# Tree attention: K and Q of heads 16 to 79 laid side by side by GpSimd, 18 output buffers, another order of the products with V

## The chip, the cores and the metric

One core of one Trainium2 chip runs the whole kernel. The metric is device time in microseconds of one execution. The names of the engines are those of the profile: PE is TensorE (matrix products; PEld its weight loads), DVE is VectorE, ACT is ScalarE, POOL is GpSimd, SP is SyncE. POOL also issues most of the DMA transfers.

## What is computed

Attention over 8 x 12 = 96 heads with 512 positions of 64 numbers each, under a mask that is a tree: position i sees itself and its ancestors (parent (i - 1) // 2).

```python
mask = np.zeros((seq, seq))
for i in range(seq):
    mask[i, i] = 1
    parent = i
    while parent > 0:
        parent = (parent - 1) // 2
        mask[i, parent] = 1
scores = np.einsum('bhqd,bhkd->bhqk', Q, K) * scale + (1 - mask) * (-1e9)
weights = np.exp(scores - np.max(scores, axis=-1, keepdims=True))
weights = weights / (np.sum(weights, axis=-1, keepdims=True) + 1e-10)
return np.einsum('bhqk,bhkd->bhqd', weights, V).astype(np.float32)
```

All inputs and the output are fp32 in device memory.

## The kernel before

**Pairs.** The 96 heads are worked as 48 pairs; in a pair, one head lies in partitions 0 to 63 and the other in 64 to 127 wherever the 64 dimensions lie on the partitions. One iteration of the main loop (line 860) takes the scores of pair i ("S": scores1 and scores2), the products with V of pair i - 1 ("V": values and norm), and turns (transposes) K or Q of later pairs ("K", "Q"). Pairs 0 to 7 are turned one by one, pairs from 8 (WIDE) on by two. From pair 8 on K comes in odd iterations and Q in even ones, apart from the first iterations, whose order is written out in FIRST (line 856). There, iteration 6 is 'SKDVQ': scores of pair 6, then K of pairs 8 and 9 is turned. Later, iteration i turns Q of pairs i + 4 and i + 5 if it is even, and K of i + 3 and i + 4 if it is odd. "D" and "A" are the places where VectorE and ScalarE spread V.

**The mask** enters through codes: each score tile begins with a product of two code matrices (L567, L601) that adds a large negative number where the tree forbids, and the product of Q and K is added on top (L574, L612). scores1 makes the 512 queries' scores with the 128 topmost keys (tile s1, exponential into e1), scores2 the rest (tile s2, exponentials into e2). s1, s2 and the output tile ob have one PSUM buffer each, so that the next pair's scores wait for the exponentials of the pair before.

**Loads.** K, Q and V come as bf16 (the DMA casts from fp32) in blocks: K and Q in blocks b of 8 heads (4 buffers each), V in blocks of 16 heads (3 buffers). They are all issued by POOL, in the order of pool_program (line 720), mixed with POOL's share of spreading V (spread_top, spread_pool: copies from the loaded rows vst to the tiles vt, L371) and with the stores (L702). POOL works its list strictly in order; pool(i) only says after which iteration an instruction is put into the program, which fixes which readers of a buffer a new load has to wait for.

**Turning.** A turn brings 8 slots of two heads from rows to columns by products with an identity matrix. For pairs 8 to 39 each slot takes two transposes, one for each head, with 64 columns of the array each (L477 for K, L507 and L538 for Q): 16 of them. For blocks 10 and 11 (heads 80 to 95, pairs 40 to 47) lay_beside has POOL copy a block so that the two heads of each slot lie side by side (L445), and a slot then takes one transpose with 128 columns (L470, L532): 8 of them. VectorE takes the result out of PSUM (L486, L490, L494 for K; L515, L543 for Q).

**Products with V.** values(i) makes 20 products (L662): for each of the two heads four with e1 and two with e2, all with 128 queries, and after both heads the 8 products "halves", with 64 queries each, that end the sums. norm divides (L692, L694) into an output tile "of" of 8 heads. There are NOUT // 2 = 11 of those; a tile is free again when its store has landed.

Of the kernel before, what the change touches and what calls it, by code (L numbers as in the profile page):

```python
# [9 lines left out]

CODE = 2048.0
CODE_ROWS = 40
NOUT = 22
BEHIND = 56


# [21 lines left out]
SELF = (2, 3, 2, 3)  # L38
# [81 lines left out]
def kernel(  # L120
# [7 lines left out]
    nc = tc.nc  # L128
# [33 lines left out]

    consts = ctx.enter_context(tc.tile_pool(name="consts", bufs=1))
    loads = ctx.enter_context(tc.tile_pool(name="loads", bufs=4))
    vloads = ctx.enter_context(tc.tile_pool(name="vloads", bufs=3))
    work = ctx.enter_context(tc.tile_pool(name="work", bufs=4))
    qwork = ctx.enter_context(tc.tile_pool(name="qwork", bufs=2))
# [272 lines left out]
    def lay_beside(name, b):  # L440

        kept = ksts if name == "kst" else qsts
        assert all((name, h) in issued for h in range(KB * b, KB * b + KB))
        sides[name, b] = side = loads.tile([P, KB, 4, D], bf16, name=name)
        return nc.gpsimd.tensor_copy(  # L445
            out=side.rearrange("p (s a) t d -> p s a (t d)", a=2).rearrange(
                "p s a (t d) -> p (s a t) d", t=4
            ).rearrange("p (s a) d -> p s a d", a=2).bitcast(int32),
            in_=kept[b].rearrange("p (a x) t d -> p (x t) a d", a=2).bitcast(int32),
        )  # L450

    def both(name, i, slot):

        side = sides[name, i // 4].rearrange("p h t d -> p (h t d)")
        return side[:, 2 * D * slot:2 * D * slot + 2 * D]

    def slots(st, i):
        return st[2 * i // KB].rearrange("p (g x) t d -> p g (x t) d", x=2)

    def wide_k(i):  # L460
        kp = ktp.rearrange("p u c -> p (u c)")
        st = slots(ksts, i)
        place = [2 * i % KB // 2 + a if i < FAR else i % 4 // 2 + 2 * a for a in range(2)]
        for u in range(2):
            for t in range(4):
                mixed = 64 * MIXED[t] + 32 * u
                leaves = 512 + 64 * LEAVES[t] + 32 * u
                dims = (256, 2), (leaves - mixed, 2), (1, 32)
                if ("kst", i // 4) in sides:
                    nc.tensor.transpose(  # L470
                        out=columns(kp, mixed, *dims),
                        in_=both("kst", i, 8 * (i % 4 // 2) + 4 * u + t),
                        identity=ptile[:, 0:128],
                    )
                    continue
                for a in range(2):
                    nc.tensor.transpose(  # L477
                        out=columns(kp[64 * a:64 * a + 64, :], mixed, *dims),
                        in_=st[:, place[a], 4 * u + t, :],
                        identity=ptile[:, 0:128],  # L480
                    )
# [12 lines left out]
        nc.vector.tensor_copy(  # L494
            out=columns(flat, 0, (320, 4), (128, 2), (1, 64)),
            in_=columns(kp, 512, (128, 4), (64, 2), (1, 64)),
        )

    def wide_q(i):
        qp = qtp.rearrange("p u c -> p (u c)")  # L500
        halves = qp.rearrange("p (b c) -> p b c", b=2)
        st = slots(qsts, i)
        for u in range(2):
            for x, t in enumerate(ORDER):
                c = 256 * u + 64 * x
                for a in range(2):
                    nc.tensor.transpose(  # L507
                        out=halves[64 * a:64 * a + 64, :, c:c + 64],
                        in_=st[:, 2 * i % KB // 2 + a, 4 * u + t, :],
                        identity=ptile[:, 0:128],  # L510
                    )
# [3 lines left out]
        nc.vector.tensor_copy(  # L515
            out=qq[:, :, 0:16, :].rearrange("p b u c -> p b (u c)"), in_=halves
        )
# [3 lines left out]
    def far_q(i):  # L521
        qp = qtp.rearrange("p u c -> p (u c)")
        quarters = qp.rearrange("p (b c) -> p b c", b=4)
        j, last = i // 4, i % 4 // 2
        if not last:
            qqs[j] = qwork.tile([P, 4, 16, 32], bf16, name="qq")
        st = qsts[j].rearrange("p (g x) t d -> p g (x t) d", x=4)
        for u in range(2):
            for x, t in enumerate(ORDER):
                c = 128 * u + 32 * x  # L530
                if ("qst", j) in sides:
                    nc.tensor.transpose(  # L532
                        out=quarters[:, :, c:c + 32], in_=both("qst", i, 4 * (2 * last + u) + t),
                        identity=ptile[:, 0:128],
                    )
                    continue
                for a in range(2):
                    nc.tensor.transpose(  # L538
                        out=quarters[64 * a:64 * a + 64, :, c:c + 32],
                        in_=st[:, a, 4 * (2 * last + u) + t, :],  # L540
                        identity=ptile[:, 0:128],
                    )
        nc.vector.tensor_copy(  # L543
            out=qqs[j][:, :, 8 * last:8 * last + 8, :].rearrange("p b u c -> p b (u c)"),
            in_=quarters,
        )
        if last:
            for b in range(4):
                qTs[4 * j + b] = qqs[j][:, b, :, :].rearrange("p (t u) c -> p t (u c)", t=4)

    def turn(name, i):
        pairs = range(i, i + (2 if i >= WIDE else 1))
        if name == "qst" and i >= FAR:
            pairs = range(i - i % 4, i - i % 4 + 4)
        assert all((name, head(j, a)) in issued for j in pairs for a in range(2)), (name, i)
        level = (i >= WIDE) + (i >= FAR)
        {"kst": (narrow_k, wide_k, wide_k), "qst": (narrow_q, wide_q, far_q)}[name][level](i)
        return i + (2 if i >= WIDE else 1)

# [90 lines left out]
    def values(i):  # L650
# [15 lines left out]
                **flags,  # L666
            )

        def halves(a):
            for t in (0, 1):  # L670
                product(e2, a, t, 1 + SELF[t], 0, 64, start=False, stop=t == 1)
                product(e2, a, t, 1 + t, 64, 128, start=False, stop=t == 1)

        for a in range(2):
            for t in range(4):
                product(e1, a, t, 0, start=t == 0, stop=False)
            for t in (2, 3):
                product(e2, a, t, 1 + t, start=False, stop=False)
            if i == NP - 1:
                halves(a)  # L680
        if i < NP - 1:
            for a in range(2):
                halves(a)

# [35 lines left out]
    def pool_program():  # L720
# [6 lines left out]
            (load_q, 16, 4), (load_rows, 1, "even"), (load_k, 20, 4), (load_rows, 1, "odd"),  # L727
            (load_q, 20, 4), (load_k, 24, 8), (load_q, 24, 4), (load_rows, 2, "upper"),
            (load_q, 28, 4), (load_rows, 2, "leaves0", "leaves1"), (load_k, 32, 8), (load_q, 32, 8),
            (load_rows, 3, "upper"),  # L730
            (spread_pool, (1, "Z0", 8, 16), (1, "Z1", 8, 16), (1, 6, 8, 16), (1, 9, 8, 16)),
            (load_q, 40, 8), (load_k, 40, 8), (load_rows, 3, "leaves0", "leaves1"), (load_q, 48, 8),
            (spread_top, 2), (spread_pool, (2, "Z0", 0, 16), (2, "Z1", 0, 16)), (load_k, 48, 8),
            (spread_pool, (2, "X", 0, 16), (2, "M", 0, 16), (2, "D1", 0, 16)), (spread_top, 3, 0, 12),
            (load_rows, 4, "upper"), (spread_top, 3, 12, 16),
        ]
        loaded, stored = 72, 0
        for h in range(56, NH, KB):
            top = [(spread_top, h // VB + 0)] if h % VB == 8 and 4 <= h // VB + 0 < NH // VB else []
            if top:  # L740
                top.append((spread_pool, (h // VB, "Z0", 0, 16), (h // VB, "Z1", 0, 16)))
            ops += [(load_q, h, KB)] + top + [(load_k, h, KB)]
            if h == 64:
                ops.append((
                    spread_pool, *[(3, part, 0, 16) for part in ("Z0", "Z1", "X", "M", "D1")]
# [22 lines left out]
    def ready(op, i):  # L768
# [2 lines left out]
        if f in (load_k, load_q):  # L771
            return 2 * (i + 3) >= args[0] + args[1] - 4 * KB
        if f is lay_beside:
            return 2 * (i + 3) >= KB * (args[1] + 2) + KB - 4 * KB
        if f is load_v:
            return True
        if f is load_rows:
            return 2 * i >= VB * (args[0] - 2)
        if f is spread_pool:
            return 2 * i >= VB * (args[0][0] + 1 - NV)  # L780
        if f is spread_top:
# [145 lines left out]
```

## Time and profile before

| | |
|---|---|
| median of 3 runs | 134.0 us (133.42 to 134.24) |
| the profiled execution | 133.38 us, its span 131.6 us |
| busy, share of the span | PE 114.4 us (87%), DVE 103.8 (79%), ACT 101.1 (77%), POOL 83.0 (63%) |
| moved, by the instructions' account | 37.94 MB read from HBM, 12.58 MB written: 384 GB/s over the span |
| granted TensorE clock, mean | 0.969 |

The span runs from the first to the last instruction; the time of the execution is 1.8 us longer. Busy shares are means over stages in which different engines set the pace, so they are read together with the rows that say what each instruction waited for. A row of the chain gives a start, a length and a name; a row of the timeline gives a start, a length, the engine, the line, the operation and its tiles, and in brackets the idle time before it and what ended that. "x16" after a row means 16 instructions in one. The waits before DMA issues on POOL often end at the landing of an earlier transfer.

### The profile page before, as it was taken

What the parts mean: (1) busy time and instruction counts of PE and PEld (TensorE: products, weight loads), DVE (VectorE), ACT (ScalarE), POOL (GpSimd) and SP (SyncE); (2) the same over time, 40 slices, a digit from 0 to 9 for tenths busy, and PEclk for the clock granted to TensorE, in tenths of its full rate; (3) what the DMA queues carried; (4) which work ended last, traced back from release to release, by engine and by line L of the source; (5) the groups of instructions that cost most, each with busy time, mean ns of one, the idle gap of its engine ahead of it and who ended that gap; (6) DMA issues with size and microseconds to landing.
All of it is one profiled execution on the core that took longest, in us unless ns stands there. A gap on an engine that the chain in (4) does not pass through costs nothing.

```text
span 131.6 us, 5435 instructions
## 1 busy us (share of the span) xinstructions
PE 114.4 (87%) x2353; PEld 79.7 (61%) x2353; DVE 103.8 (79%) x254; ACT 101.1 (77%) x163; POOL 83.0 (63%) x114
## 2 busy tenths in 40 slices
PE   6788959999999798899998898997998999999900
PEld 2354745676667566577676575675675777775600
DVE  3459859588999998989899879898899977875440
ACT  4279577689799996959996878896898888789900
POOL 6999524454485999994498799944999935002000
PEclk9999996799999999999999999999999999999975
DMA  2999999999999999999999999999999999999991
GB/s 87 244 195 194 200 196 200 201 202 206 203 201 209 207 207 204 210 206 202 209 206 200 306 269 207 293 282 242 330 221 327 246 288 400 403 398 396 395 345 66
DMA packets 28157, 32.25 MB, mean 245 GB/s; under 512 B 1214, under 2 KB 23358, under 8 KB 28134
## 3 DMA queue, kind: packets, MB, share of 16 engines
q0 software_dynamic: 25696, 29.63, 110.7%
q1 hardware_dynamic: 1878, 1.83, 4.0%
q10 hardware_dynamic: 560, 0.46, 1.3%
q8 instruction: 18, 0.29, 0.8%
q14 instruction: 5, 0.04, 0.1%
HBM read 37.94 MB, written 12.58 MB: 384 GB/s over the span
## 4 chain that ended last, share of the span: by engine, by line
DMA 30%; PE 29%; POOL 17%; DVE 13%; issue 4%; ACT 2%; POOLq 0%; ACTq 0%
DMA kst<-in_K_dram 22%; PE ob L662 9%; POOL vt L371 9%; DMA vst<-in_V_dram 8%; PE s L567 4%; DVE of L694 4%; DVE vt L371 3%; PE s L574 3%; POOL kst L244 2%; POOL qst L244 2%; PE s L612 2%; PE s L601 2%; POOL vst L244 2%; PE qtp L532 2%; PE ktp L470 2%
## 5 line engine op out<-in xcount | busy, mean ns | idle before, releaser
L584 ACT ACTIVATE e<-s 128x1024 bf16<-128x1024 f32 x40 | 40.9, 1022 | 13.2 <-PE s L574 12.7
L662 PE MATMUL ob<-vt,e 128*128 128x65 bf16 (+1 forms) x940 | 37.4, 198 | 1.6 <-DVE of L694 1.1
L662 PEld LDWEIGHTS <-e 128*128 128x128 bf16 (+1 forms) x960 | 30.4, 103 | 9.5 <-PE s L612 1.1
L371 POOL COPY vt<-vst 32x512 int32<-32x512 int32 (+4 forms) x44 | 32.5, 740 | 5.2 <-PE ob L662 3.0
L618 ACT ACTIVATE e<-s 128x384 bf16<-128x384 f32 x80 | 34.7, 490 | 0.0
L694 DVE TENSOR_TENSOR of<-ob,rec 128x512 f32<-128x512 f32 x47 | 32.5, 692 | 1.6
L371 DVE COPY vt<-vst 32x1024 bf16<-32x1024 bf16 (+5 forms) x47 | 21.4, 456 | 2.6 <-DMA vst<-in_V_dram 1.8
L692 DVE RECIPROCAL rec<-ob 128x8 f32<-128x8 f32 x47 | 9.6, 205 | 10.7 <-PE ob L662 9.8
L702 POOL DMA_DIRECT2D out_dram<-of x11 | 9.9, 898 | 9.1 <-DVE of L694 8.7
L574 PE MATMUL s<-qq,kq 64*128 64x512 bf16 x80 | 15.3, 377 | 0.0
L612 PE MATMUL s<-qq,kq 64*128 64x160 bf16 (+1 forms) x320 | 14.8, 208 | 0.4 <-issue 0.4
L612 PEld LDWEIGHTS <-kq 64*128 64x128 bf16 x320 | 12.3, 94 | 4.7 <-issue 0.6
L567 PE MATMUL s<-far,codes 40*128 40x512 bf16 x64 | 12.5, 386 | 0.1
L580 ACT ACTIVATE e<-s 128x1024 bf16<-128x1024 f32 x8 | 8.2, 1022 | 5.6 <-PE s L574 5.5
L254 POOL DMA_DIRECT2D qst<-in_Q_dram x12 | 8.4, 704 | 6.3 <-DMA kst<-in_K_dram 3.4
L601 PEld LDWEIGHTS <-codes 40*128 40x128 bf16 x80 | 6.4, 94 | 9.5 <-issue 3.9
L543 DVE COPY qq<-qtp 128x1024 bf16<-128x1024 bf16 x16 | 10.9, 682 | 0.7 <-PE qtp L538 0.7
L254 POOL DMA_DIRECT2D kst<-in_K_dram x11 | 8.4, 764 | 4.3 <-DMA vst<-in_V_dram 1.7
L477 PE MATMUL ktp<-ptile,kst 128*64 128x128 bf16 x256 | 9.9, 220 | 1.2 <-DMA kst<-in_K_dram 0.6
L601 PE MATMUL s<-far,codes 40*128 40x384 bf16 x64 | 10.6, 324 | 0.4 <-ACT e L618 0.3
L371 ACT COPY vt<-vst 32x512 int32<-32x512 int32 (+3 forms) x19 | 10.4, 546 | 0.6 <-DMA vst<-in_V_dram 0.2
L299 POOL DMA_DIRECT2D vst<-in_V_dram x7 | 5.6, 800 | 6.4 <-DMA vst<-in_V_dram 4.5
(56 smaller groups left out, 157.2 us busy)
## 6 DMA issues: line engine op xcount, KB each, us to landing
out_dram<-of POOLq DMA_DIRECT2D x10, 1024.0 KB, 16.4
kst<-in_K_dram POOLq DMA_DIRECT2D x9, 512.0 KB, 14.3
qst<-in_Q_dram POOLq DMA_DIRECT2D x8, 512.0 KB, 16.3
vst<-in_V_dram POOLq DMA_DIRECT2D x12, 256.0 KB, 14.0
vst<-in_V_dram POOLq DMA_DIRECT2D x6, 512.0 KB, 13.0
qst<-in_Q_dram POOLq DMA_DIRECT2D x6, 256.0 KB, 12.1
kst<-in_K_dram POOLq DMA_DIRECT2D x4, 256.0 KB, 10.8
out_dram<-of SPq DMA_DIRECT2D x3, 256.0 KB, 6.0
```

Source lines behind the costliest of these rows:

```text
L254: return nc.gpsimd.dma_start(out=kept[b][:, h0 % KB:h0 % KB + n, :, :].rearrange("p (g x) t d -> p g (x t d)", x=x), in_=src[:, h0 // x:(h ...
L371: return copy(out=dst, in_=src)
L477: nc.tensor.transpose(out=columns(kp[64 * a:64 * a + 64, :], mixed, *dims), in_=st[:, place[a], 4 * u + t, :], identity=ptile[:, 0:128],)
L543: nc.vector.tensor_copy(out=qqs[j][:, :, 8 * last:8 * last + 8, :].rearrange("p b u c -> p b (u c)"), in_=quarters,)
L567: nc.tensor.matmul(out=sp[:, a, :], lhsT=(k1code if i < WIDE else k1wide)[64 * a:64 * a + CODE_ROWS, :], rhs=(q1code, q1wide, q1far)[(i >= ...
L574: nc.tensor.matmul(out=sp[:, a, :], lhsT=keys(i, a, TOP), rhs=qTs[i][64 * a:64 * a + 64, :, :].rearrange("p t c -> p (t c)"), start=False, ...
L584: ) if i < WIDE else nc.scalar.activation(
L601: nc.tensor.matmul(out=flat[:, a, :, :].rearrange("p u (t c) -> p u t c", t=4)[:, :, :, 32 // n:], lhsT=k2wide[64 * a:64 * a + CODE_ROWS, ...
L612: nc.tensor.matmul(out=flat[:, a, :, lo:hi], lhsT=keys(i, a, WTILE2[t]), rhs=qT[64 * a:64 * a + 64, :, lo:hi], start=False, stop=t == 1, s ...
L618: nc.scalar.activation(out=e2s[i % NE][:, a, :, 32:128].rearrange("p t (r u) -> p t r u", u=n), in_=flat[:, a, :, :].rearrange("p u (t r) ...
L662: nc.tensor.matmul(out=ob[lo:hi, a, 65 * t:65 * t + 65], lhsT=e[:, a, PLACE[t], lo:hi], rhs=vt[vtile[tile_v][0]][:, head(i, a) % VB, vtile ...
L694: nc.vector.tensor_tensor(out=ofs[j][:, h0:h1 + 1:head(i, 1) - head(i, 0), :, :], in0=o4[:, a:a + n, :, 0:D], in1=rec[:, a:a + n, :, :].to ...
```

## The change

It has four parts. POOL lays K and Q of blocks 2 to 9 (heads 16 to 79) side by side too, into a pool "beside" of its own with two buffers for each of K and Q; blocks 2 and 3 in two half copies each. All pairs from 8 on are then turned by 8 transposes with 128 columns. The copies stand at given places of POOL's list, behind loads and spreads; the load of Q of heads 56 to 63 moves ahead of some spreads and of the upper rows of V block 4, and the conditions under which entries of the list may be put into the program are adapted. The output tiles go from 11 to 9. In values, for pairs 8 to 46, the half products come first (and start the sums), and the products with 128 queries follow.

```diff
-NOUT = 22
+NOUT = 18
...
+    beside = ctx.enter_context(tc.tile_pool(name="beside", bufs=2))
...
-        sides[name, b] = side = loads.tile([P, KB, 4, D], bf16, name=name)
-        return nc.gpsimd.tensor_copy(
...
+        sides[name, b] = side = beside.tile([P, 16, 2, D], bf16, name=f"{name}side")
+        if KB * b >= 2 * FAR:
+            return nc.gpsimd.tensor_copy(
+                out=side.bitcast(int32),
+                in_=kept[b].rearrange("p (a x) t d -> p (x t) a d", a=2).bitcast(int32),
+            )
+        for m in range(2):
+            nc.gpsimd.tensor_copy(
+                out=side[:, 8 * m:8 * m + 8, :, :].bitcast(int32),
+                in_=kept[b][:, 4 * m:4 * m + 4, :, :].rearrange(
+                    "p (a x) t d -> p (x t) a d", a=2
+                ).bitcast(int32),
+            )
...
     def wide_k(i):
...
-                for a in range(2):
-                    nc.tensor.transpose(
-                        out=columns(kp[64 * a:64 * a + 64, :], mixed, *dims),
-                        in_=st[:, place[a], 4 * u + t, :],
-                        identity=ptile[:, 0:128],
-                    )
+                nc.tensor.transpose(
+                    out=columns(kp, mixed, (256, 2), (leaves - mixed, 2), (1, 32)),
+                    in_=both("kst", i, 8 * (i % 4 // 2) + 4 * u + t),
+                    identity=ptile[:, 0:128],
+                )
...
-        def halves(a):
+        def halves(a, start=False):
             for t in (0, 1):
-                product(e2, a, t, 1 + SELF[t], 0, 64, start=False, stop=t == 1)
-                product(e2, a, t, 1 + t, 64, 128, start=False, stop=t == 1)
-
+                for tile_v, lo in ((1 + SELF[t], 0), (1 + t, 64)):
+                    product(
+                        e2, a, t, tile_v, lo, lo + 64, start=start and t == 0,
+                        stop=not start and t == 1,
+                    )
+
+        first = i >= WIDE and i < NP - 1
+        if first:
+            for a in range(2):
+                halves(a, True)
         for a in range(2):
             for t in range(4):
-                product(e1, a, t, 0, start=t == 0, stop=False)
+                product(e1, a, t, 0, start=t == 0 and not first, stop=False)
             for t in (2, 3):
-                product(e2, a, t, 1 + t, start=False, stop=False)
+                product(e2, a, t, 1 + t, start=False, stop=first and t == 3)
             if i == NP - 1:
                 halves(a)
-        if i < NP - 1:
+        if i < NP - 1 and not first:
...
             (load_q, 28, 4), (load_rows, 2, "leaves0", "leaves1"), (load_k, 32, 8), (load_q, 32, 8),
-            (load_rows, 3, "upper"),
+            (lay_beside, "kst", 2), (lay_beside, "qst", 2), (load_rows, 3, "upper"),
             (spread_pool, (1, "Z0", 8, 16), (1, "Z1", 8, 16), (1, 6, 8, 16), (1, 9, 8, 16)),
-            (load_q, 40, 8), (load_k, 40, 8), (load_rows, 3, "leaves0", "leaves1"), (load_q, 48, 8),
+            (load_q, 40, 8), (load_k, 40, 8), (lay_beside, "kst", 3), (lay_beside, "qst", 3),
+            (load_rows, 3, "leaves0", "leaves1"), (load_q, 48, 8),
             (spread_top, 2), (spread_pool, (2, "Z0", 0, 16), (2, "Z1", 0, 16)), (load_k, 48, 8),
-            (spread_pool, (2, "X", 0, 16), (2, "M", 0, 16), (2, "D1", 0, 16)), (spread_top, 3, 0, 12),
+            (lay_beside, "kst", 4), (lay_beside, "qst", 4),
+            (spread_pool, (2, "X", 0, 16), (2, "M", 0, 16), (2, "D1", 0, 16)),
+            (load_q, 56, 8), (lay_beside, "qst", 5), (lay_beside, "kst", 5), (spread_top, 3, 0, 12),
             (load_rows, 4, "upper"), (spread_top, 3, 12, 16),
...
-            ops += [(load_q, h, KB)] + top + [(load_k, h, KB)]
+            beside = [(lay_beside, name, h // KB - 2) for name in ("qst", "kst")]
+            ops += ([(load_q, h, KB)] + beside if h > 56 else []) + top + [(load_k, h, KB)]
...
         if f is lay_beside:
-            return 2 * (i + 3) >= KB * (args[1] + 2) + KB - 4 * KB
+            return args[1] < 4 or i >= 4 * args[1] - 8
...
         if f is load_rows:
-            return 2 * i >= VB * (args[0] - 2)
+            return i >= {4: 12, 5: 17}.get(args[0], 8 * (args[0] - 2))
```

wide_q and far_q change like wide_k: one transpose of a slot from the copied tile in place of two from the loaded one.

More of the change, by code (lines that the diff above doesn't have):

```diff
@@ L443, in lay_beside @@
         assert all((name, h) in issued for h in range(KB * b, KB * b + KB))
-        sides[name, b] = side = loads.tile([P, KB, 4, D], bf16, name=name)
[L445 to L449, printed above, removed]
-        )
+        sides[name, b] = side = beside.tile([P, 16, 2, D], bf16, name=f"{name}side")
[11 more added lines that the diff above has]
+            )
     def both(name, i, slot):
[L454 to L458, printed above, removed]
+        return sides[name, i // 4][:, slot, :, :].rearrange("p a d -> p (a d)")
     def wide_k(i):
         kp = ktp.rearrange("p u c -> p (u c)")
-        st = slots(ksts, i)
-        place = [2 * i % KB // 2 + a if i < FAR else i % 4 // 2 + 2 * a for a in range(2)]
         for u in range(2):
@@ L467, in wide_k @@
                 leaves = 512 + 64 * LEAVES[t] + 32 * u
[L468 to L472, printed above, removed]
-                        identity=ptile[:, 0:128],
-                    )
-                    continue
-                for a in range(2):
-                    nc.tensor.transpose(
-                        out=columns(kp[64 * a:64 * a + 64, :], mixed, *dims),
-                        in_=st[:, place[a], 4 * u + t, :],
-                        identity=ptile[:, 0:128],
-                    )
+                nc.tensor.transpose(
[3 more added lines that the diff above has]
+                )
         kk = work.tile([P, 2, 20, 32], bf16, name="kq")
@@ L501, in wide_q @@
         halves = qp.rearrange("p (b c) -> p b c", b=2)
-        st = slots(qsts, i)
         for u in range(2):
@@ L505, in wide_q @@
                 c = 256 * u + 64 * x
[L506 to L511, printed above, removed]
+                nc.tensor.transpose(
+                    out=halves[:, :, c:c + 64], in_=both("qst", i, 8 * (i % 4 // 2) + 4 * u + t),
+                    identity=ptile[:, 0:128],
+                )
         qq = qwork.tile([P, 4, 16, 32], bf16, name="qq")[:, 0:2, :, :]
@@ L526, in far_q @@
             qqs[j] = qwork.tile([P, 4, 16, 32], bf16, name="qq")
-        st = qsts[j].rearrange("p (g x) t d -> p g (x t) d", x=4)
         for u in range(2):
@@ L530, in far_q @@
                 c = 128 * u + 32 * x
[L531 to L542, printed above, removed]
+                nc.tensor.transpose(
+                    out=quarters[:, :, c:c + 32], in_=both("qst", i, 4 * (2 * last + u) + t),
+                    identity=ptile[:, 0:128],
+                )
         nc.vector.tensor_copy(
@@ L556, in turn @@
         level = (i >= WIDE) + (i >= FAR)
+        assert not level or (name, i // 4) in sides, (name, i)
         {"kst": (narrow_k, wide_k, wide_k), "qst": (narrow_q, wide_q, far_q)}[name][level](i)
@@ L667, in product @@
             )
-        def halves(a):
+        def halves(a, start=False):
             for t in (0, 1):
-                product(e2, a, t, 1 + SELF[t], 0, 64, start=False, stop=t == 1)
-                product(e2, a, t, 1 + t, 64, 128, start=False, stop=t == 1)
+                for tile_v, lo in ((1 + SELF[t], 0), (1 + t, 64)):
+                    product(
+                        e2, a, t, tile_v, lo, lo + 64, start=start and t == 0,
+                        stop=not start and t == 1,
+                    )
+        first = i >= WIDE and i < NP - 1
+        if first:
+            for a in range(2):
+                halves(a, True)
         for a in range(2):
             for t in range(4):
-                product(e1, a, t, 0, start=t == 0, stop=False)
+                product(e1, a, t, 0, start=t == 0 and not first, stop=False)
             for t in (2, 3):
-                product(e2, a, t, 1 + t, start=False, stop=False)
+                product(e2, a, t, 1 + t, start=False, stop=first and t == 3)
             if i == NP - 1:
                 halves(a)
-        if i < NP - 1:
+        if i < NP - 1 and not first:
             for a in range(2):
```

## The prediction

> **What bounds the kernel now.** I read the page first, for the busy shares and the DMA row.
>
> ```profile
> span 131.6 us, 5435 instructions
> PE 114.4 (87%) x2353; PEld 79.7 (61%) x2353; DVE 103.8 (79%) x254; ACT 101.1 (77%) x163; POOL 83.0 (63%) x114
> DMA  2999999999999999999999999999999999999991
> HBM read 37.94 MB, written 12.58 MB: 384 GB/s over the span
> ```
>
> The transfers never pause. 37.94 + 12.58 = 50.52 MB, and the change moves the same bytes. Cutting the span into 5 us stretches (busy time of PE, PEld, DVE, ACT, POOL; then clock, DMA share, GB/s counted on the receiving side) gives their rate:
>
> ```profile
> 5.00:10.00 5.00, 3.65 (x61) 2.32 (x56) 2.80 (x7) 3.55 (x5) 5.00 (x8) 1.00 1.45 195
> 110.00:115.00 5.00, 5.00 (x95) 3.67 (x94) 4.04 (x10) 4.09 (x8) 1.02 (x2) 1.00 1.04 400
> ```
>
> Early, 195 GB/s of bf16 arrive from twice as many fp32 bytes, that is 390 GB/s read; late, 400 GB/s of stores leave. 50.52 MB at 400 GB/s is 126.3 us of the 131.6. A gain could come only out of the remaining 5.3 us, most of which is the first landing and the last store. So I ask not what the change speeds up, but whether something falls behind the transfers. For that I read the chain that ended last, in order of time (start, us, what):
>
> ```profile
> 84.00 0.64 PE ktp L477 x16
> ...
> 90.39 0.61 POOL vt L371
> ...
> 99.85 1.05 POOL qst L445
> ...
> 126.15 0.42 DVE of L694
> ```
>
> The end hangs on POOL already: POOL spreads V of heads 80 to 95 from 90.39 on, lays Q of heads 80 to 87 side by side at 99.85, TensorE takes that at its end, and from there pair follows pair to the last normalization. Whatever moves the 90.39 moves the end by as much. Last, POOL's instructions in order of time:
>
> ```profile
> 30.65 0.77 POOL L254 DMA_DIRECT2D kst<-in_K_dram  x1 [1.01 <-DVE qq L515]
> 31.93 0.70 POOL L254 DMA_DIRECT2D qst<-in_Q_dram  x1 [0.51 <-PE s L612]
> 34.52 0.85 POOL L299 DMA_DIRECT2D vst<-in_V_dram  x1 [1.89 <-ACT vt L371]
> 84.04 0.70 POOL L254 DMA_DIRECT2D qst<-in_Q_dram  x1
> 90.39 2.59 POOL L371 COPY vt<-vst 32x512 int32<-32x512 int32 x4 [3.04 <-PE ob L662]
> ```
>
> The 31.93 issue is the load of Q of heads 32 to 39, the 34.52 one the upper rows of V block 3, the 84.04 one Q of heads 80 to 87.
>
> **The change, part by part.**
>
> *The copies.* The diff adds lay_beside for blocks 2 to 9 (8 heads each), K and Q: 8 half copies for blocks 2 and 3, and 12 whole ones. Both sizes have rows (grouped by shape: busy, mean ns of one):
>
> ```profile
> L445 POOL COPY kst<-kst 128x1024 int32<-128x1024 int32 x2 | 2.1, 1046 | 1.7 <-DMA kst<-in_K_dram 1.7
> L371 POOL COPY vt<-vst 32x1024 int32<-32x1024 int32 x16 | 17.3, 1079 | 0.8
> L371 POOL COPY vt<-vst 32x512 int32<-32x512 int32 x18 | 11.2, 621 | 3.9 <-PE ob L662 3.0
> ```
>
> A whole copy is 1.05 us; 32 and 128 partitions cost the same at 1024 elements, so I give a half (128x512) 0.62. With the 0.05 us that stands between copies (17.3 busy, 0.8 idle, 16 copies), 12 x 1.1 + 8 x 0.67 = 18.6 us of new work on POOL, in a fixed order, most of it where POOL is fullest.
>
> *The first wait.* TensorE turns K of pair 8 within iteration 6, and needs no copy for it today:
>
> ```profile
> 26.98 0.64 PE L477 MATMUL ktp<-ptile,kst 128*64 128x128 bf16 x16
> 28.76 0.29 DVE L371 COPY vt<-vst 64x512 bf16<-64x512 bf16 x1
> 28.94 0.38 PE L574 MATMUL s<-kq 64*128 64x512 bf16 x2
> ```
>
> After the change it reads the copy of block 2, and POOL's program puts that behind the Q load issued at 31.93, which waits as now (nothing ahead of it changes). So the first half copy runs 32.65 to 33.3, and the turn starts at 33.3 instead of 26.98: 6.3 us in which TensorE stands still, with scores, products and transposes of all later pairs queued behind it in order. VectorE's copies of that turn and the spreads behind them stop too, ScalarE has no scores to take. Pair 7's scores, 28.94 now, come near 35.2. The loads go on meanwhile.
>
> *The long stretch on POOL.* After four halves (2.7 us) POOL is at 35.3. The load of V block 3 then waits for the buffer of block 0, whose last spread on VectorE (28.76, done 29.05, 2.07 us behind the turn's start) now ends at 33.3 + 2.07 = 35.4. So that load, at 34.52 before, is issued at 35.5. From there to the Q load that ends at 84.74 POOL does the same work as before:
>
> ```profile
> 34.52:84.74 50.22, 46.26 (x1066) 33.52 (x1064) 45.64 (x107) 43.38 (x73) 41.65 (x59) 1.00 1.24 219
> ```
>
> The fifth number, 41.65 us of 50.22, is POOL. Idle time that could take in copies is 8.6 us at most, of which some 1.8 us are those 0.05 us steps (35 copies stand there). Into this stretch go 4 halves of block 3 and, for blocks 4 to 7, 8 whole copies, and after the 84.04 load comes Q of block 8, a ninth: 4 x 0.67 + 9 x 1.1 = 12.6 us. Filled without any wait, POOL ends that copy at 35.5 + 41.65 + 1.8 + 12.6 = 91.5. What they read has landed long before: the loads of blocks 4 to 7 are issued two blocks ahead. The load of Q of heads 56 to 63 is only moved ahead of some spreads; its issue (0.70) is in the 41.65.
>
> *What is late next.* Q of block 8 is turned in iteration 28. In the trace the scores of the pair after that turn are the first row here; the hand-over of the whole copy of 99.85 ended in the second, and the third is the pair behind it:
>
> ```profile
> 82.26 0.38 PE L574 MATMUL s<-qq,kq 64*128 64x512 bf16 x2
> 101.72 0.38 PE L574 MATMUL s<-qq,kq 64*128 64x512 bf16 x2
> 103.90 0.38 PE L574 MATMUL s<-qq,kq 64*128 64x512 bf16 x2
> ```
>
> 99.85 + 1.05 = 100.90 to 101.72 is 0.8 us from a copy's end to the scores. So pair 29 starts at 92.3 instead of 82.26: 10.0 us late. From 82.26 to 90.39, when POOL's wait for the products of pair 31 ends, there are 8.1 us, with a wait for K of heads 64 to 71 in it (the 84.00 of the chain) that is no wait any more; I take 0.4 us off. POOL meets that point early (K of 8, two loads, a store, Q and K of 9: 91.5 + 5.6 = 97.1), waits until 90.39 + 9.6 = 100.0, and from there everything is as in the chain above.
>
> *The transposes.* Half as many, twice as wide. The group starts show what that is worth (values, turn, next codes; the first three with 16 narrow ones, then with 8 wide):
>
> ```profile
> 45.07 0.77 PE L662 MATMUL ob<-vt,e 128*128 128x65 bf16 x20 [0.62 <-DVE of L694]
> 45.68 0.61 PE L477 MATMUL ktp<-ptile,kst 128*64 128x128 bf16 x16
> 46.23 0.40 PE L567 MATMUL s<-codes 40*128 40x512 bf16 x2
> 102.40 0.79 PE L662 MATMUL ob<-vt,e 128*128 128x65 bf16 x20
> 103.12 0.62 PE L470 MATMUL ktp<-ptile,kst 128*128 128x128 bf16 x8
> 103.67 0.39 PE L567 MATMUL s<-far,codes 40*128 40x512 bf16 x2
> ```
>
> Both turns last 0.55 us: no gain. But ahead of the wide turn the products last 0.72 instead of 0.61, and the products now end in half-column ones.
>
> *The order of the products.* It lets full-width products stand next to the wide turn. At best this returns the 0.11 us in each pair from 37 on that still has a turn (7 of them, 0.8 us); at worst the other border, scores to half-column products, costs as much. I take 0.4 us off, ends -0.8 and +0.8. It adds no wait: the half products need the second exponentials, and these are done by then, since the next pair's scores need their PSUM:
>
> ```profile
> 119.27 0.34 PE L601 MATMUL s<-far,codes 40*128 40x384 bf16 x2 [0.15 <-ACT e L618]
> ```
>
> *Two output buffers fewer* (11 tiles of 8 heads to 9): the tenth tile is first written by pair 36, after the 101.72 scores of pair 37, and needs the store of heads 0 to 7, issued at 59.84 now and near 67 then, with 16.4 us to landing:
>
> ```profile
> 59.84 0.91 POOL L702 DMA_DIRECT2D out_dram<-of  x1
> out_dram<-of POOLq DMA_DIRECT2D x10, 1024.0 KB, 16.4
> ```
>
> That lands near 83, some 20 us early; the eleventh and twelfth tiles follow each 4 pairs, like the stores. Nothing; without that cover VectorE would wait in norm and TensorE behind it.
>
> *Sum.* The profiled execution took 133.38 us (its span of 131.6 and 1.8 around it), 0.6 under the median of 134.0. 133.4 + 10.0 - 0.4 - 0.4 = 142.6 us.
>
> **Rivals.**
>
> *A: POOL finds room.* The copies of blocks 4 to 9 fit into its waits and only the first wait counts. Then pair 7 is 6.3 us late and the pairs catch up as they can. Up to 50 us they cannot:
>
> ```profile
> 35.00:50.00 15.00, 13.55 (x310) 9.72 (x310) 14.57 (x36) 14.74 (x25) 12.35 (x19) 1.00 1.27 206
> ```
>
> VectorE is busy 14.57 and ScalarE 14.74 of 15 us. Pair 14, whose codes are the 46.23 row, is then still 6.3 late at 52.5; 23 pairs on, at 2.25 us each (2.18 from the rows 101.72 and 103.90, and 0.07 estimated for the spreads), pair 37 has its codes at 104.3 and its scores 0.2 later, 104.5 against 101.72. That is 2.8 late: 136.2. Against it: 12.6 us of copies and 8.6 us of idle time on POOL.
>
> *B: not slower.* The transfers are the bound, and pairs wait for loads at several places (the 84.00 turn waits for its K). If the pairs made up the whole 6.3 us between 52.5 and 101.5, the end would be where the transfers put it, 133.4. It decides once 23 pairs take 49.0 us, 2.13 each, which needs the 0.11 us of the product order back in nearly every pair, no other stall, and a POOL that is never late. The transfers' slack lets it go no lower than about 133.
>
> *C: the delays feed each other.* TensorE's clock is halved after a stall (0.51 in the row below, early in this trace), POOL's copies run slower beside a busier VectorE, and the last loads, issued some 10 us later, find the queue empty.
>
> ```profile
> 21.00:24.50 3.50, 3.50 (x36) 1.68 (x35) 2.73 (x7) 2.30 (x4) 1.48 (x2) 0.51 1.40 202
> 49.85 1.25 POOL vt L371
> ```
>
> With 0.51 of the clock the turn at 33.3 and the spread behind it come up to 0.6 us later, which POOL's load of V block 3 inherits; at 1.25 instead of 1.05 us nine whole copies add 1.8, four halves 0.5; an empty queue at the last stores 1 us. Together 3.9: 146.5. The Trainium skill (TensorE: Matmul & The Clock Gate, Part 1) says that an idle window of about 3.4 us halves TensorE's clock and a busy one restores it; the 21 to 24.5 row agrees in length, and by that rule a 6.3 us stall would bring one such window for certain. The Trainium skill (GPSIMD Engine Reference, Key points) also says that GpSimd shares its SBUF interfaces with VectorE and contends with some of its instructions; the mean rows of 1046 and 1079 ns show little of it, the single 1.25 us copy perhaps some.
>
> **How the numbers follow.** Forecast 0.71, A 0.14, C 0.11, B 0.04. The range goes from 135.6 (A, with 0.6 of the product order's best) to 147.3 (C, with 0.8 on its worst side), which leaves out B and the tails. A measurement of this kernel tells about 1% (1.3 us) from no change. Faster by over 1%: 0.01, since the transfers leave no room. Within 1%: 0.04, which is B. Slower: 0.95.
>
> **What would show it.** Right: a TensorE wait of about 6 us near 27, ended by POOL's copy on kst; POOL without idle time from 35 to some 97 us; pair 29's scores near 92, behind the copy of qst; POOL waiting for the products of pair 31 until about 99 to 100; the stores crowding later, with the DMA row below 9 in places. Wrong: a turn of pair 8 that starts before 32; POOL's Q copy of block 8 before 85 or after 95; a pair spacing well under 2.1 us with wide turns; or a wait of norm for a store.

## The result and the profile after

The changed kernel takes 146.84 us (median of 6 runs, 145.65 to 148.33) against 133.78 us before (6 runs): a ratio of 1.096, 95% interval 1.092 to 1.100. The prediction said 142.6 us, between 135.6 and 147.3.

The lines below are from a second profile of the changed kernel, an execution of 147.33 us (span 145.6). From its page: the engines, POOL, TensorE's clock and the DMA row, each digit a fortieth of the span.

```profile
PE 118.1 (81%) x2094; PEld 82.4 (57%) x2097; DVE 108.0 (74%) x254; ACT 101.2 (69%) x163; POOL 100.2 (69%) x134
POOL 7979352556999999949999999992099995010200
PEclk9999999955699999999999999857999968999998
DMA  4999999999999999999999999999961999994294
```

POOL has 17.2 us more work (83.0 before) and is full from the eleventh digit to the 27th, but for one digit. The DMA row, nine throughout before, has holes: the transfers are no longer the bound. TensorE's clock dips three times. POOL's instructions in order of time:

```profile
32.10 0.70 POOL L255 DMA_DIRECT2D qst<-in_Q_dram  x1 [0.50 <-issue]
32.80 1.17 POOL L452 COPY kstside<-kst 128x512 int32<-128x512 int32 x2
33.90 1.16 POOL L452 COPY qstside<-qst 128x512 int32<-128x512 int32 x2
36.47 0.85 POOL L300 DMA_DIRECT2D vst<-in_V_dram  x1 [1.40 <-issue]
...
63.88 1.45 POOL L372 COPY vt<-vst 32x128 int32<-32x128 int32 x4 [1.82 <-PE ob L643]
...
92.71 1.03 POOL L447 COPY qstside<-qst 128x1024 int32<-128x1024 int32 x1
...
105.23 4.81 POOL L372 COPY vt<-vst 32x512 int32<-32x512 int32 x6 [6.17 <-PE ob L643]
```

These answer to the 31.93, 34.52 and 90.39 rows of before. The first copies stand behind the Q load, as the list says; a copy of 1024 elements takes 1.03 us, one of 512 about 0.6. Between 36.47 and 92.71 POOL waits once for long, 1.82 us. TensorE, in the same order:

```profile
25.58 0.36 PE L620 MATMUL s<-kq 64*128 64x160 bf16 x8
33.48 1.03 PE L469 MATMUL ktp<-ptile,kstside 128*128 128x128 bf16 x8 [7.54 <-POOL kstside L452]
...
36.83 0.64 PE L555 MATMUL s<-kq 64*128 64x512 bf16 x2
...
93.80 1.03 PE L519 MATMUL qtp<-ptile,qstside 128*128 128x128 bf16 x8 [2.57 <-POOL qstside L447]
95.16 0.64 PE L555 MATMUL s<-qq,kq 64*128 64x512 bf16 x2
98.81 0.64 PE L555 MATMUL s<-qq,kq 64*128 64x512 bf16 x2
101.58 0.38 PE L555 MATMUL s<-qq,kq 64*128 64x512 bf16 x2
```

The turn of pair 8 waits 7.54 us for the copy, and the turn behind the copy of Q of block 8 waits 2.57 us. Pair 29's scores come at 95.16 (82.26 before). A turn takes 1.03 us in both places where it took 0.62: TensorE runs at half its clock. Two stretches of the profile show this (busy time of PE, PEld, DVE, ACT, POOL; clock, DMA share, GB/s):

```profile
28.70:38.90 10.20, 5.42 (x64) 4.10 (x66) 2.78 (x7) 1.34 (x2) 6.62 (x11) 0.50 1.30 203
93.60:100.40 6.80, 6.60 (x72) 4.35 (x72) 4.04 (x8) 3.26 (x5) 5.46 (x7) 0.50 1.12 284
```

### The profile page after: what moved, and what is told of

The parts are those of the page before. It is cut to its first block, busy times and chain, and to the rows that moved or that the text cites. A ratio compares the mean times of both kernels' runs of the same rounds, so it can differ in the third digit from the quotient of the medians.

```text
span 146.6 us, 4941 instructions
## 1 busy us (share of the span) xinstructions
PE 119.4 (82%) x2097; PEld 83.0 (57%) x2097; DVE 109.9 (75%) x254; ACT 101.1 (69%) x163; POOL 100.4 (69%) x134
## 4 chain that ended last, share of the span: by engine, by line
POOL 30%; PE 26%; DMA 22%; DVE 14%; issue 4%; ACT 3%; ACTq 0%; POOLq 0%
DMA vst<-in_V_dram 17%; POOL vt L372 14%; PE ob L643 8%; DVE vt L372 5%; DMA kst<-in_K_dram 5%; PE s L548 4%; DVE of L682 4%; PE qtp L519 3%; POOL qstside L447 3%; PE s L555 3%; PE ktp L469 3%; PE s L593 2%; PE s L582 2%; POOL out_dram L690 2%; POOL kst L255 2%
## 5 line engine op out<-in xcount | busy, mean ns | idle before, releaser
L565 ACT ACTIVATE e<-s 128x1024 bf16<-128x1024 f32 x40 | 40.9, 1024 | 22.6 <-PE s L555 22.4
L643 PE MATMUL ob<-vt,e 128*128 128x65 bf16 (+1 forms) x940 | 39.1, 201 | 5.4 <-DVE of L682 3.6
L643 PEld LDWEIGHTS <-e 128*128 128x128 bf16 (+1 forms) x960 | 31.8, 105 | 13.5 <-DVE of L682 4.7
L372 DVE COPY vt<-vst 32x1024 bf16<-32x1024 bf16 (+5 forms) x47 | 27.7, 588 | 3.0 <-DMA vst<-in_V_dram 2.2
L469 PE MATMUL ktp<-ptile,kstside 128*128 128x128 bf16 x160 | 13.5, 233 | 8.6 <-POOL kstside L452 8.0
L690 POOL DMA_DIRECT2D out_dram<-of x11 | 9.8, 891 | 12.9 <-DVE of L682 12.9
L555 PE MATMUL s<-qq,kq 64*128 64x512 bf16 x80 | 16.3, 402 | 0.0
L593 PEld LDWEIGHTS <-kq 64*128 64x128 bf16 x320 | 13.0, 99 | 5.6 <-issue 1.8
L593 PE MATMUL s<-qq,kq 64*128 64x160 bf16 (+1 forms) x320 | 15.6, 217 | 0.0
L469 PEld LDWEIGHTS <-kstside 128*128 128x128 bf16 x160 | 10.4, 105 | 8.9 <-POOL kstside L452 8.1
L478 DVE COPY kq<-ktp 128x256 bf16<-128x256 bf16 x20 | 8.3, 416 | 8.8 <-PE ktp L469 8.7
L519 PE MATMUL qtp<-ptile,qstside 128*128 128x128 bf16 x128 | 10.6, 230 | 4.3 <-POOL qstside L447 4.3
L582 PEld LDWEIGHTS <-codes 40*128 40x128 bf16 x80 | 6.2, 100 | 10.2 <-issue 4.3
```

Source lines behind the costliest of these rows:

```text
L372: return copy(out=dst, in_=src)
L469: nc.tensor.transpose(out=columns(kp, mixed, (256, 2), (leaves - mixed, 2), (1, 32)), in_=both("kst", i, 8 * (i % 4 // 2) + 4 * u + t), id ...
L519: nc.tensor.transpose(out=quarters[:, :, c:c + 32], in_=both("qst", i, 4 * (2 * last + u) + t), identity=ptile[:, 0:128],)
L555: nc.tensor.matmul(out=sp[:, a, :], lhsT=keys(i, a, TOP), rhs=qTs[i][64 * a:64 * a + 64, :, :].rearrange("p t c -> p (t c)"), start=False, ...
L565: ) if i < WIDE else nc.scalar.activation(
L582: nc.tensor.matmul(out=flat[:, a, :, :].rearrange("p u (t c) -> p u t c", t=4)[:, :, :, 32 // n:], lhsT=k2wide[64 * a:64 * a + CODE_ROWS, ...
```

## The experiments

All ratios are against the kernel before in the same session; its medians there were 133.5 to 133.8 us.

**Parts that cost nothing.** The kernel before with `NOUT = 18` alone:

> The kernel before with 9 output tiles of 8 heads instead of 11, nothing else. Theory 1: the store of heads 0 to 7 has landed 20 us before the tenth tile is written: 133.8 us, no change. Rival (norm waits for a store): a wait of VectorE behind pair 36 and 135 us or more.

Measured: 0.999, interval 0.997 to 1.002. The two output tiles were never missed.

The kernel before with the new `values` alone (the diff's last part, nothing of the copies):

> The kernel before with the new order of the products with V alone (pairs 8 to 46). Theory 1: next to narrow turns the order loses the 0.11 us per pair that products of half width and narrow turns share, and wins it in the 7 pairs next to wide turns; the transfers hide most of it: 133 to 135 us, tail pace of pairs 37 to 43 at 2.07 us instead of 2.18. Theory 3 (the order itself slows TensorE): 136 or more.

Measured: 1.000, interval 0.998 to 1.002. Scores of pairs 37 to 39, around wide turns, in this run:

```profile
101.69 0.38 PE L574 MATMUL s<-qq,kq 64*128 64x512 bf16 x2
103.76 0.38 PE L574 MATMUL s<-qq,kq 64*128 64x512 bf16 x2
105.87 0.38 PE L574 MATMUL s<-qq,kq 64*128 64x512 bf16 x2
```

They stand 2.07 and 2.11 us apart (before, 101.72 to 103.90: 2.18), and the last pair's scores come 0.6 us earlier than before; the end does not move (span 131.5 against 131.6). With TensorE done earlier the time stays, which fits a kernel that the transfers bind. Next to narrow turns the new order costs what it gives next to wide ones: in this run pairs 34 to 36 stand 2.20 and 2.18 us apart (94.73, 96.93 and 99.11), in the kernel before 2.07 and 2.11 (94.64, 96.71 and 98.82). The runs below that keep narrow turns with the new order carry this too.

**The two suspects apart.** A switch chooses the blocks that are copied and read (`USED` decides between the old pair of narrow transposes and the wide one):

```diff
...
-    program = pool_program()
+    program = [op for op in pool_program() if op[0] is not lay_beside or op[2] in LAID]
```

Blocks 2 and 3 (and 10 and 11, as before) alone:

> The changed kernel with the copies of blocks 4 to 9 left out: pairs 16 to 39 are turned from the loaded tiles as in the kernel before; blocks 2, 3, 10 and 11 are copied. Theory 1 (two causes: the first wait at the turn of pair 8, and POOL's list that is longer than the time it has): the first wait stays (some 7 us near 26), then the pairs catch up part of it, 136 to 139 us. Theory 2 (the first wait alone makes the loss, and the rest only passes it on): 145 to 147. Theory 3 (TensorE is slower per pair with wide turns and the new order of products, the copies are hidden): 134 to 135.

Measured: 1.060 (1.049 to 1.072), 8.1 us. Blocks 4 to 11 alone:

> The changed kernel with the copies of blocks 2 and 3 left out: pairs 8 to 15 are turned from the loaded tiles; blocks 4 to 11 are copied. Theory 1: no wait near 26, but POOL still reaches its Q copy of block 8 late, near 87 instead of 95, so that the scores of pair 29 come near 88 instead of 82: 138 to 141 us. Theory 2: 134 us. Theory 3: 144 to 147.

Measured: 1.066 (1.059 to 1.073), 8.8 us. Each half costs about two thirds of it: neither theory 2 nor theory 3 fits both runs, and my theory 1 was too low in both, by 2.6 us in the first (141.6 by the ratio) and 1.3 us in the second. Together they cost 12.9 us and not 8 + 9. The second run's trace shows one reason: its first copy that is read, K of block 4, brings a wait of its own, which theory 1 had not expected.

```profile
49.78 1.04 PE L485 MATMUL ktp<-ptile,kstside 128*128 128x128 bf16 x8 [5.53 <-POOL kstside L449]
```

In the changed kernel TensorE waits for no copy between pair 8's turn and 91 us; its pairs come there late already. So each half pays a first wait, and the whole pays one.

**POOL's time without the hand-over.** All copies are made, but pairs 8 to 39 are turned from the loaded tiles:

> The changed kernel with all its copies on POOL, but TensorE reads only those of blocks 10 and 11; pairs 8 to 39 are turned from the loaded tiles. Theory 1, with POOL's time itself as the cost: no TensorE wait for a copy before block 10, but POOL comes to the spreads of heads 80 to 95 near 97 instead of 90 and so to Q of block 10 near 107: 138 to 141 us. If only the hand-over to TensorE costs (a copy on the way of each turn, and POOL has room): 133.5 to 135.

Measured: 1.030 (1.022 to 1.038), 4.0 us, a little under what was expected. POOL waits for nothing from 44 us to the spread of V block 5 and comes to it late all the same, as the chain that ended last shows (start, us, what):

```profile
93.89 1.05 POOL qstside L449
94.94 0.98 POOL kstside L449
95.97 0.60 POOL vt L374
...
105.40 1.05 POOL qstside L449
106.50 0.62 PE qtp L552 x8
```

95.97 against 90.39 before, +5.6; the span is 136.6, +5.0. So 4 of the 13 us come from POOL's time without any hand-over. The other 9 need TensorE to read the copies.

**The place in the list.** The changed kernel with the halves of block 2 moved up:

```diff
...
-            (load_q, 20, 4), (load_k, 24, 8), (load_q, 24, 4), (load_rows, 2, "upper"),
-            (load_q, 28, 4), (load_rows, 2, "leaves0", "leaves1"), (load_k, 32, 8), (load_q, 32, 8),
-            (lay_beside, "kst", 2), (lay_beside, "qst", 2), (load_rows, 3, "upper"),
+            (load_q, 20, 4), (load_k, 24, 8), (load_q, 24, 4), (lay_half, "kst", 0), (load_rows, 2, "upper"),
+            (load_q, 28, 4), (lay_half, "qst", 0), (load_rows, 2, "leaves0", "leaves1"),
+            (lay_half, "kst", 1), (load_k, 32, 8), (load_q, 32, 8), (lay_half, "qst", 1),
+            (load_rows, 3, "upper"),
...
```

> The changed kernel with the four half copies of block 2 moved up in POOL's list, each behind the load issue by which its data have about landed (first half of K ahead of the upper rows of V block 2). Theory 1: the wait near 26 shrinks from 8 us to under 2, POOL is the bound from 35 on with its list as long as before: 140 to 143 us. Theory 2: 134 to 136. Theory 3: 145 to 147.

Measured: 1.074 (1.064 to 1.083), 9.9 us, or 143.4 by the ratio, a little over what theory 1 gave. Its turns of pair 8, K and Q:

```profile
26.63 0.62 PE L481 MATMUL ktp<-ptile,kstside 128*128 128x128 bf16 x8
28.52 0.62 PE L509 MATMUL qtp<-ptile,qstside 128*128 128x128 bf16 x8 [0.66 <-POOL qstside L446]
```

The 7.5 us wait is gone and the turn runs at 0.62 us; of that the end gains 3.0 us (9.9 late instead of 12.9). From 35 us on POOL's list is the bound, as theory 1 says; TensorE's waits have moved to later copies (3.69 us at 40.47 for K of block 3, 3.67 us at 90.56 for Q of block 8).

**Half of the copies.** K alone, with the first halves early:

> The changed kernel with only K of blocks 2 to 9 copied, half of POOL's new work (the first halves moved up in its list as in the run with early halves), and Q of pairs 8 to 39 turned from the loaded tiles. If POOL's time is the cost: its 9.3 us of copies go mostly into the 8.6 us that it was idle between 34.5 and 84.7, 134.5 to 137 us. If the hand-over of each copy to TensorE is the cost, half of the 9 to 10 us of the run with early halves: 138 to 139.

Measured: 1.032 (1.023 to 1.040), 4.2 us. By the ratio this is 137.9 us, between the two expectations. One row of the list of waits in its profile (an execution of 139.79 us; who waited for whom: us in total, times, longest) stands out:

```profile
PE ktp L497 <- POOL kstside L466: 5.4, 1, 5.4
```

It is one wait, for K of block 3, and ends at 40.25. So 9.3 us of POOL work are enough to lose a third of the 12.9 us once TensorE reads them.

**A delay by itself.** The kernel before, with idle products in front of the turn of pair 8 and no copies at all:

```diff
...
-    FIRST = ['KSQ', 'SXKQXDVAKQ', 'SVKQ', 'SKQAV', 'KSVXQA', 'SAKQVDW', 'SKDVQ', 'SVD', 'SVDKQX']
+    FIRST = ['KSQ', 'SXKQXDVAKQ', 'SVKQ', 'SKQAV', 'KSVXQA', 'SAKQVDW', 'SXXXXXXXXXXXXXXXXKDVQ', 'SVD', 'SVDKQX']
...
```

This is the run with 32 products; the one with 14 has seven X.

> The kernel before with 32 idle matmuls of 512 columns in front of the turn of pair 8, no copies, nothing else: TensorE gives its pairs nothing for some 7 us, but stays busy and at full clock. Theory 4 (a delay of the pairs at 27 us is not won back, because spreads, buffers and with them POOL's loads follow the pairs and the transfers run dry): pair 28 some 7 to 9 us later, 139 to 142 us. Rival, the prediction's: pairs win back more than half, 136 to 137.

> As the stall of 7 us, with 14 idle matmuls: about 3 us. Theory 4: some 3 us, less what the transfers in the queue cover, 135 to 137 us. Rival: under 1 us, 133.5 to 134.5.

The idle products ran at 0.3 us each, not 0.2, so the delays were longer than meant: pair 7's scores came 9.4 us later than before with 32 of them and 4.3 us later with 14 (38.36 and 33.21 against 28.94). Measured: 1.066 (1.056 to 1.076), that is 8.8 us; and 1.024 (1.014 to 1.034), 3.2 us. Most of a delay arrives at the end (8.8 of 9.4 us, and 3.2 of 4.3, with 1.8 to 4.5 in the interval), with the clock at 0.99 and no new copy on POOL. POOL and the transfers in the longer one:

```profile
31.69 0.70 POOL L254 DMA_DIRECT2D qst<-in_Q_dram  x1 [0.35 <-PE s L848]
39.01 0.85 POOL L299 DMA_DIRECT2D vst<-in_V_dram  x1 [6.62 <-DVE rec L692]
...
58.27 2.67 POOL L371 COPY vt<-vst 32x384 int32<-32x384 int32 x4 [4.03 <-PE ob L662]
...
81.47 4.82 POOL L371 COPY vt<-vst 32x512 int32<-32x512 int32 x6 [2.95 <-PE ob L662]
...
100.34 4.87 POOL L371 COPY vt<-vst 32x512 int32<-32x512 int32 x6 [6.26 <-PE ob L662]
```

Each of POOL's waits is for the late pairs: 6.62 us for the buffer of V block 0 and then, at each block of V, for the products that still read the tiles which the next block overwrites. Loads stand behind those waits, and the queue of transfers runs low. The same 5 us of the stalled kernel and, second, of the kernel before:

```profile
60.00:65.00 5.00, 4.82 (x116) 3.55 (x115) 4.55 (x12) 3.71 (x7) 3.14 (x8) 1.00 0.86 113
60.00:65.00 5.00, 4.84 (x124) 3.60 (x122) 4.35 (x12) 4.95 (x10) 1.45 (x2) 1.00 1.33 204
```

113 GB/s arrive instead of 204, and the stream does not make it up in the 20 us behind it: in the next four stretches of 5 us it moves 157, 199, 257 and 233 GB/s where the kernel before moves 206, 245, 272 and 240.

**The clock.** The same idle products in the changed kernel:

> The changed kernel with 32 idle matmuls of 512 columns in front of the turn of pair 8, so that TensorE is busy through most of its first wait. If the halved clock behind that wait costs something of its own: no half clock near 28 to 36, the load of V block 3 about 1 us earlier and the end 0.5 to 1.5 us earlier, 145.3 to 146.3. If not: 146.8, as the changed kernel.

Measured: 1.102 (1.092 to 1.110), 13.6 us, no better. The run does not settle what the clock costs: its idle products ended late, and the turn came at 38.15, 4.7 us behind the 33.48 of the changed kernel. That the end did not come later too fits a gain from the full clock (mean 0.98 against 0.93), but is not shown.

**The order in the changed kernel.** Its new `values` taken back:

> The changed kernel with the old order of the products. Theory 1: POOL is the bound, so the middle does not change; the tail from pair 37 on goes back from 2.07 to 2.18 us a pair, 0.7 us in all: 147 to 148. Theory 3: 2 us or more faster than the changed kernel, 144 or less.

Measured: 1.085 (1.078 to 1.092), 11.4 us late instead of 12.9, where I expected a loss of 0.7; theory 3's 144 or less is just outside the interval, whose lower end is 144.2. Its pairs 29 and 37 come at 94.68 and 115.89, within 0.7 us of the changed kernel; then this run had no dip of the clock, while the profile shown above has this one:

```profile
117.50:120.90 3.40, 3.40 (x44) 2.32 (x42) 3.07 (x6) 1.99 (x4) 3.40 (x5) 0.50 0.97 366
```

In the 3.41 us ahead of that dip (114.06 to 117.47) TensorE was busy for 1.68 us; in this run the stretch of that length at the same place, counted in steps of 3.41 us from its own dips (113.06 to 116.47), has 1.94. Whether that is due to the order stays open.

**Once more.** 

> The changed kernel once more, for a second profile: 146 to 147 us, with the first wait near 26, Q of block 8 copied near 95 and POOL's wait for the products of pair 31 until 104 to 106.

Measured: 147.33 us, a little over what was expected; it is the profile shown above. POOL ended its copy at 93.74, and its wait ended at 105.23. No run points to a version that beats the kernel before.

## Why the prediction was right, and what was mis-sized

The bound, the place, the engine and the order of events were right; 142.6 was 4.2 us below the measured median of 146.8, and 4.7 us below the execution of the profile shown. By the prediction's own steps (that profile, in us):

| step | predicted | measured |
|---|---|---|
| turn of pair 8 starts | 33.3 | 33.48 |
| scores of pair 7 | 35.2 | 36.83 |
| load of V block 3 issued | 35.5 | 36.47 |
| copy of Q of block 8 ends | 91.5 | 93.74 |
| scores of pair 29 | 92.3 | 95.16 |
| products of pair 31 release POOL | 100.0 | 105.23 |
| from there to the end of the span | 40.8 | 40.4 |

**The first wait.** Right to 0.2 us. It is 7.54 us long instead of 6.3 only because TensorE came there earlier in this execution.

**POOL's list.** The sum of its rows held: 35.5 to 91.5 was 56.0 us, measured 36.47 to 93.74, 57.3. The 1.3 us more come from the wait of 1.82 us at 63.88 that "filled without any wait" left out: POOL may overwrite tiles of V only behind the late products of pair 15. The run with unread copies, in which POOL did not wait, shows the sum by itself: 35.30 to 90.39, 55.1 us.

**The clock is the term that was mis-sized.** The sum had nothing for it; rival C gave it 0.6 us, once, at the first turn. It came three times (10.2, 6.8 and 3.4 us at half the clock), and the second dip stood on the path that sets the end. In the first, VectorE's spread of V block 0 ended at 35.94, 2.46 us behind the turn's start and not 2.07: 0.4 us. In the second, it took 1.4 us from the copy's end to the scores instead of 0.8, and pairs 29 and 30 took 3.65 and 2.77 us instead of some 2.2 (the first profile, of 148.33 us, has the same two figures): 2.6 us. Together this is 3.0 of the 4.7 us missing. POOL's wait above makes 1.3. Another 0.4 is the time from the end of VectorE's spread to the load of V block 3, which the prediction put at 0.1 us: it is 0.53 here (35.94 to 36.47), and 0.53 in the stalled kernel too (38.48 to 39.01).

The Trainium skill (TensorE: Matmul & The Clock Gate, Part 1) states windows of some 3.4 us; the dips here last one, two and three of these. It calls the windows free-running. The trace agrees: the dips start at 28.72, 93.57 and 117.47, that is 19 and 7 windows of 3.41 us apart. So the prediction's "for certain" was too strong: 6.3 us are less than two windows and need not hold a whole one. Nor did a window have to be idle: the second dip came behind a wait of 2.57 us, and in the window before it (90.16 to 93.57) TensorE was busy for 0.87 us. That a short wait can bring it stood in the waits of before, where the one of TensorE ahead of its dip was shorter still:

```profile
PE ktp L409 <- DMA kst<-in_K_dram: 1.5, 1, 1.5
```

All 14 traces together say how short. They hold 494 such windows at full clock with a further window behind them, counted from each run's own dips. All 22 in which TensorE was busy for 53% of the window or less were followed by half the clock, and none of the 440 with 67% or more; in between it was 5 of 32.

**The last step agrees by luck.** Pairs 37 to 47 took 1.5 us longer than before (116.57 to 138.81 against 101.72 to 122.50), with the third dip among them. But the span ended 2.7 us behind VectorE's last instruction instead of 5.0.

**Rival C's total is luck too.** Its 146.5 is nearer to the measured time than the forecast, but not by its sum. The 2.3 us for slower copies on POOL did not come (1.03 to 1.07 us for a whole copy, apart from single ones), and the end grew shorter where C had it 1 us longer. Only its clock was there, five times as large as its 0.6 us.

**Rival A had a false step.** Pair 7 was 7.9 us late and not 6.3, mostly for the clock. And A let a late pair catch up, because before the pairs took 2.40 us (46.23 to 101.5, 23 pairs) where 2.18 would do. The stalls show that they do not (in the longer one pair 37's scores come at 111.72, 10.0 us late): what held them back before were loads and the spreads of V, and these follow the pairs when the pairs are late. "The loads go on meanwhile" was true for some 30 us and then false. The run with blocks 2 and 3 alone, 8.1 us late where A gave 2.8, is close to that step by itself, though its narrow turns stand next to the new order.

**The rest.** Buffers: nothing, as said. The order of the products gave 0.07 to 0.11 us a pair next to wide turns, as far as the best end of its bounds, took about as much next to narrow ones, and left the time of the kernel before where it was. Rival B (not slower) is excluded by the unread copies: POOL has no room for them even when nobody waits.

## What to carry to other kernels

Where one in-order queue both issues the loads and does copies, look up what stands ahead of a new copy in that queue before asking how long the copy takes: here 1 us of copying stood behind a load that was not issued before 32 us. In a kernel whose transfers are saturated from end to end, a delay of the compute has no slack to vanish into as soon as buffers tie the loads to the compute, so price it at its full length (here 8.8 of 9.4 us arrived). Half as many instructions are no gain until two rows show the groups themselves taking less time.

## What the runs showed of the hardware

**POOL's queue.** In all 14 traces, no transfer that POOL issues starts sooner than 0.28 us after the landing of the eighth one before it, and in each trace 12 to 19 of them start 0.28 to 0.32 us after it. No run tests such a limit by itself, but it fits the late place of the Q load, which came 0.57 us after such a landing in the kernel before (31.36 to 31.93) and 0.57 in the changed one (31.52 to 32.10). By this a copy that stands behind a load in POOL's list waits for that landing too.

**VectorE and POOL.** VectorE slows beside POOL's copies, but here only where both sides of its copy lie in SBUF. The spreads of V on VectorE, grouped by line (busy, mean ns of one), in the kernel before and in the run with unread copies:

```profile
L371 DVE COPY vt<-vst 32x1024 bf16<-32x1024 bf16 (+5 forms) x47 | 21.4, 456 | 2.6 <-DMA vst<-in_V_dram 1.8
L374 DVE COPY vt<-vst 32x1024 bf16<-32x1024 bf16 (+5 forms) x47 | 26.9, 573 | 3.3 <-DMA vst<-in_V_dram 2.4
```

The same 47 copies cost 5.5 us more. Two of them in the kernel before show it one by one, the first while POOL copies (from 80.30 on), the second as its copies end (the next store is issued at 83.13):

```profile
80.70 0.91 DVE L371 COPY vt<-vst 32x1024 bf16<-32x1024 bf16 x1
83.06 0.42 DVE L371 COPY vt<-vst 32x1024 bf16<-32x1024 bf16 x1
```

In that kernel, the 8 of the 47 that overlap no work of POOL take at most 0.42 us; beside POOL's copies they take up to 0.91, and beside its issues of transfers up to 0.89.

Copies out of PSUM did not change; of these two rows the first is of the kernel before, the second of the changed one:

```profile
L486 DVE COPY kq<-ktp 128x256 bf16<-128x256 bf16 x20 | 8.3, 417 | 0.3 <-PE ktp L477 0.3
L478 DVE COPY kq<-ktp 128x256 bf16<-128x256 bf16 x20 | 8.3, 416 | 8.2 <-PE ktp L469 8.2
```

The prediction looked for this on POOL's side, where a whole copy stayed at 1.03 to 1.07 us apart from single ones (1.30 at 70.64). The Trainium skill (GPSIMD Engine Reference, Key points) says that the two share SBUF interfaces and contend in some of VectorE's modes; the runs agree, and here it is VectorE that pays nearly all of it. What part of the 4 us of the unread copies goes through this was not separated.
